# A two-layer encoder in fp32: the feed-forward moves to row order, its tokens are normalised in place from pair 3 on, and GpSimd's pair splits come in halves

## The chip, the cores and the metric

The kernel runs on one core of a Trainium2 chip (trn2). The metric is the device time of one execution in microseconds (us), the median of three runs. Engines are named as the profile names them: PE is TensorE's matmuls, PEld its weight loads, DVE VectorE, ACT ScalarE, POOL GpSimd, SP SyncE, which issues nearly all DMAs.

## What is computed

Two layers on 512 tokens (8 rows of 64 columns) of width 1024, each with three residual parts, and a last RMSNorm. Cut to what matters here:

```python
def conv_ffn(h, w_up, conv_w, conv_b, w_down):
    u = h @ w_up                                  # 1024 -> 2 x 2816
    up = jnp.pad(u, ((0, 0), (1, 1), (0, 0)))
    u = up[:, :-2] * conv_w[0] + up[:, 1:-1] * conv_w[1] + up[:, 2:] * conv_w[2] + conv_b
    gate, val = jnp.split(u, 2, axis=-1)
    return (jax.nn.silu(gate) * val) @ w_down

for l in range(DEPTH):                            # DEPTH = 2
    x = x + hybrid_mixer(rms_norm(x, norm_mix[l]), ...)      # neighbourhood and grouped-query attention
    x = x + memory_cross_attention(rms_norm(x, norm_mem_q[l]), rms_norm(mem, norm_mem_kv[l]), ...)
    x = x + conv_ffn(rms_norm(x, norm_ffn[l]), w_up[l], conv_w[l], conv_b[l], w_down[l])
return rms_norm(x, norm_final)
```

The convolution runs along the token index, which counts along a row of 64 columns first.

## The kernel before

Everything is held transposed: xT is eight chunks of 128 channels by 512 tokens. The tokens stand column by column (token = column x 8 + row), as the neighbourhood attention wants them, from the first load to the result, which the host puts back. In that order a token's neighbour in a row lies 8 elements away, and the first one of a row follows the last one of the row before across the whole tile. So each of the convolution's two outer taps is two instructions on VectorE (line 1826): one of 504 elements and one of 7.

Each fp32 matmul is made of three: both operands are split into a high part that TensorE takes as it is (ScalarE copies it, type fp32r) and a low part, the rest (VectorE or GpSimd subtracts), and high x high, high x low and low x high are added up in PSUM (`mm3`, `gemm_T`). The weights are split on the way in: `split_form` (line 746) does it for those of the forms described below, the low part on GpSimd or VectorE.

`Norm` keeps a residual's normalisation. When an output row m (128 channels) of the memory attention (`mem_rows`) or of the last part of the first layer's feed-forward (`down_closing`) is done in PSUM, `close` adds xT[m] in PSUM (line 974), copies the sum to xT[m] (975), makes the high part on ScalarE (983) and the low part on VectorE (985) of the sum times the gain, into the tiles `xg`, and squares it (ScalarE, added up by GpSimd). The reciprocal root of the mean square is not known then; it is multiplied in later.

The feed-forward of a layer goes over 22 pairs of column blocks (128 gate columns and 128 value columns each), in groups of 6, 6, 5 and 5; between the pairs of a group the rows of `down` for the group before are computed. Pairs 0 to 5 (`PLAIN` = 6) are plain products: `up_project` for both sides from `xg`, then `up_finish` multiplies both by the spread reciprocal root `ffn.rep` (line 1809), then `convolve`: ScalarE does the middle tap with the bias, VectorE the outer taps, ScalarE the SiLU, VectorE the product, and the result is split for `down`.

From pair 6 on `up_forms` computes a pair by seven products of half the tokens and half the channels instead of eight. It needs normalised tokens and sums of them, so in pairs 2 to 5 `token_forms` makes xn = xT x gain x reciprocal root (line 1846, eight chunks in four tiles) and then four sums and differences of quarters of it, t1, t3, t2 and t4, each split (lines 1856 to 1859); just before pair 6 `split_tokens` splits xn itself (lines 1870 and 1871) over the tiles `xg`, which the plain pairs no longer need. In `up_forms` the accumulator `first` is read by the addition on line 1903 and then written further by the last product ("val" with t4); that product waits for the addition.

The order of the instructions on ScalarE, VectorE, GpSimd and TensorE is not the order of this text. A planner (class `Order`, line 328) runs a model of the engines with costs by operation and size, and fixes each engine's order when the kernel is built. Its costs know nothing of the step between elements. SyncE's DMAs stay in the written order.

Of the kernel before, what the change touches and what calls it, by code (L numbers as in the profile page):

```python
# [20 lines left out]
S = 512  # L21
D = 1024
DEPTH = 2
GW = 64
# [13 lines left out]
PLAIN = 6  # L38
FIRST_ROWS = 2
# [614 lines left out]
def encoder_kernel(ctx: ExitStack, tc: tile.TileContext, t: dict, out: bass.AP):  # L654
# [91 lines left out]
    def split_form(src, n, act, eng):  # L746
        hi = wpool.tile([P, 2 * n, P], F32R, tag="hi", name=nm("hi"), padded_shape=[P, KC, P])
        lo = wpool.tile([P, 2 * n, P], F32R, tag="lo", name=nm("lo"), padded_shape=[P, KC, P])
        act.copy(hi, src)  # L749
        eng.tensor_sub(lo, src, f(hi))  # L750
        return hi, lo
# [207 lines left out]
    class Norm:  # L959


        def __init__(self, gcol=None, l=None, cols=slice(0, S)):
            self.gcol, self.l, self.acc, self.last, self.cols, self.n = gcol, l, None, [], cols, cols.stop - cols.start
            if gcol is not None:
                self.hi, self.lo = [xpool.tile([P, KC, S], F32R, tag="xg", name=nm("xg"), bufs=2) for _ in range(2)]
                self.ops = [(self.hi[:, c, :], self.lo[:, c, :]) for c in range(KC)]
# [4 lines left out]
        def close(self, c, pm):  # L971


            DVE.tensor_add(pm, pm, xT[c])
            DVE.tensor_copy(xT[c], pm)
            self.operand(c, src=pm)
            self.square(c)

        def operand(self, c, act=ACT, src=None, dve=DVE, hi_only=False, lo_only=False):
            src = xT[c] if src is None else src  # L980
            g = self.gain(c)
            hi, lo = self.ops[c]
            e = None if lo_only else act.activation(hi, src, AF.Copy, scale=g)
            if not hi_only:
                dve.scalar_tensor_tensor(lo, src, g, f(hi), op0=ALU.mult, op1=ALU.subtract)
            return e
# [162 lines left out]
    for l in range(DEPTH):  # L1149
# [615 lines left out]
        nn = Norm(G_FFN, l)  # L1765
# [35 lines left out]
        def up(j):  # L1801
            if j >= PLAIN:
                up_forms(j)
                return
            up_finish(j, [up_project(j, side) for side in range(2)])
# [6 lines left out]
        def convolve(j, us):  # L1812
            cs = []
            for side in range(2):
# [5 lines left out]
                for wi, dst, src in (  # L1820
                    (w[0], slice(8, S), slice(0, S - 8)),
                    (w[0], slice(1, 8), slice(S - 8, S - 1)),
                    (w[2], slice(0, S - 8), slice(8, S)),
                    (w[2], slice(S - 8, S - 1), slice(1, 8)),
                ):
# [15 lines left out]
        def token_forms():  # L1841
# [3 lines left out]
            for c in range(KC):  # L1845
                DVE.scalar_tensor_tensor(xn[c // 2][:, c % 2], xT[c], ffn.gain(c), ffn.psum, op0=ALU.mult, op1=ALU.mult)
                if c == 3:
                    yield
            yield
            made = {}  # L1850
            for name, a, b in (("t1", (0, 1), (0, 0)), ("t3", (1, 1), (0, 1)), ("t2", (1, 1), "t1"), ("t4", (1, 0), "t2")):
# [9 lines left out]

        def split_tokens():


            for name, k, n in (("b11", 0, 0), ("b21", 1, 0), ("b22", 1, 1)):
                xform[name] = [v[:, 4 * k : 4 * k + 4, halves[n]] for v in (ffn.hi, ffn.lo)]
            for c, n in ((0, HALF), (2, HALF), (4, S), (6, S)):
                hi, lo = (v[:, c : c + 2, :n] for v in (ffn.hi, ffn.lo))
                src = xn[c // 2][:, :, :n]
                ACT.copy(hi, src)  # L1870
                DVE.tensor_sub(lo, src, f(hi))  # L1871
# [108 lines left out]
        for what, n, rows in sequence():  # L1980
            if what == "down":
                down(n, rows)
            elif n == 0:
                up_first()
            elif n > 1:
                if n < PLAIN:
                    next(forms, None)
                elif n == PLAIN:
                    for _ in forms:
                        pass  # L1990
                    split_tokens()
                up(n)
        if l + 1 < DEPTH:
            nn = Norm(G_MIX, l + 1)
# [88 lines left out]
```

## Time and profile before

| | |
|---|---|
| median of 3 runs | 1325.12 us (1324.66 to 1325.38) |
| profiled execution, its own time | 1324.98 us |
| span of that execution, first to last instruction | 1323.2 us |
| TensorE busy | 1306.0 us, 99% |
| VectorE / ScalarE / GpSimd busy | 1004.2 / 783.4 / 724.9 us |
| granted TensorE clock, mean | 0.996 |
| HBM traffic | 97 GB/s over the span |

The page and the views of the trace give start and length of instructions in us from the span's start, the line in the kernel, the operation, output and inputs by the program's names, sizes as partitions x elements, and in brackets how long the engine was idle before and what ended that. In a view by groups the columns are count, busy us, mean ns of one, and idle us before them. A busy TensorE is one with matmuls in flight, not one at its peak rate.

### The profile page before, as it was taken

The page shows a single profiled execution, that of the slowest core. Times are in us where ns is not written, and L with a number is a line of the kernel's source. Part 1 is how long each engine was busy: PE and PEld are TensorE (multiplying, and loading weights), DVE is VectorE, ACT ScalarE, POOL GpSimd, SP SyncE. Part 2 cuts the span into 40 slices and gives each one's busy share as a digit, 9 for nine tenths or more (in the row PEclk, how much of TensorE's full clock was granted, in tenths as well). Part 3 has the DMA queues.
Part 4 walks back from the last instruction along what each step waited for, and adds up shares of the span by engine and source line. Part 5 has one row for each costly group of instructions (what it writes and reads, how often), then busy time and mean ns, then how long its engine had stood idle before and what let it go on. Part 6 is the DMA issues. An engine that isn't in the chain of part 4 may idle for free.

```text
span 1323.2 us, 21017 instructions
## 1 busy us (share of the span) xinstructions
PE 1306.0 (99%) x7632; PEld 1150.3 (87%) x7632; DVE 1004.2 (76%) x1862; ACT 783.4 (59%) x1450; POOL 724.9 (55%) x520
## 2 busy tenths in 40 slices
PE   9999999999999999999999999999999899999998
PEld 8888888888879999999888888888888899999987
DVE  7569877665998987788545698786758998877874
ACT  6768776565555555555536688765645455555544
POOL 3657965717464544454646579655454544444443
PEclk9999999999999999999999999999999999999999
DMA  8734222313213333333455533232232233333332
GB/s 245 188 120 133 97 79 65 99 44 112 88 50 97 106 112 103 99 101 93 137 156 165 150 90 96 56 89 80 64 90 74 69 108 104 101 97 93 116 98 76
DMA packets 205000, 136.98 MB, mean 104 GB/s; under 512 B 5600, under 2 KB 195040, under 8 KB 204896
## 3 DMA queue, kind: packets, MB, share of 16 engines
q1 hardware_dynamic: 204080, 134.98, 34.7%
q8 instruction: 60, 0.98, 0.3%
q10 hardware_dynamic: 816, 0.66, 0.2%
q14 instruction: 44, 0.36, 0.1%
HBM read 125.65 MB, written 2.10 MB: 97 GB/s over the span
## 4 chain that ended last, share of the span: by engine, by line
PE 91%; DVE 5%; ACT 2%; DMA 1%; issue 1%; POOL 0%; POOLq 0%; SPq 0%; ACTq 0%; DVEq 0%
PE mm L101 62%; PE sc L101 21%; PE tr L101 4%; PE tr L1533 2%; DVE xg L1871 1%; PE tr L1378 1%; DVE r L1856 1%; DMA r<-in_bias 1%; DVE r L1031 1%; PE tr L1720 1%; DMA raw<-in_w_in 0%; ACT t L1356 0%; DVE r L1248 0%; DVE sc L1350 0%; ACT r L1227 0%
## 5 line engine op out<-in xcount | busy, mean ns | idle before, releaser
L741 POOL TENSOR_TENSOR lo<-raw,hi 128x512 fp32r<-128x512 f32 (+3 forms) x230 | 371.3, 1629 | 291.2 <-ACT hi L740 243.5
L101 PE MATMUL mm<-r,hi 128*128 128x512 f32 (+1 forms) x1392 | 398.8, 367 | 0.0
L101 PEld LDWEIGHTS mm<-r,hi 128*128 128x128 f32 x1392 | 245.7, 190 | 34.9
L101 PE MATMUL mm<-xg,hi 128*128 128x512 f32 (+1 forms) x960 | 266.5, 363 | 0.5 <-ACT t L1897 0.3
L101 PE MATMUL mm<-r,lo 128*128 128x512 f32 (+1 forms) x728 | 257.9, 356 | 0.0
L740 ACT CAST hi<-raw 128x512 fp32r<-128x512 f32 (+3 forms) x234 | 167.9, 739 | 130.0 <-PE mm L101 52.3
L101 PEld LDWEIGHTS mm<-xg,hi 128*128 128x128 f32 x960 | 170.5, 189 | 27.3 <-issue 1.0
L101 PE MATMUL mm<-xg,lo 128*128 128x512 f32 (+1 forms) x480 | 173.5, 361 | 0.0
L101 PE MATMUL sc<-r,hi 128*128 128x256 f32 (+1 forms) x832 | 165.9, 294 | 5.7 <-DVE sc L1903 5.0
L750 POOL TENSOR_TENSOR lo<-sf,hi 128x1024 fp32r<-128x1024 f32 x32 | 79.1, 2473 | 140.2 <-ACT hi L749 117.0
L101 PEld LDWEIGHTS mm<-r,lo 128*128 128x128 f32 x728 | 137.9, 189 | 19.8
L101 PEld LDWEIGHTS sc<-r,hi 128*128 128x128 f32 x832 | 135.6, 193 | 12.2 <-issue 3.1
L101 PE MATMUL sc<-r,lo 128*128 128x256 f32 (+1 forms) x416 | 122.0, 293 | 0.0
L101 PE MATMUL mm<-hi,xg 128*128 128x512 f32 (+1 forms) x384 | 111.5, 360 | 2.6 <-DVE r L1231 1.3
L749 ACT CAST hi<-sf 128x1024 fp32r<-128x1024 f32 x64 | 67.1, 1050 | 78.8 <-DVE sf L762 46.3
L750 POOL TENSOR_TENSOR lo<-raw,hi 128x1024 fp32r<-128x1024 f32 x32 | 78.1, 2439 | 47.9 <-ACT hi L749 32.9
L101 PEld LDWEIGHTS mm<-xg,lo 128*128 128x128 f32 x480 | 90.6, 189 | 14.2 <-POOL lo L750 0.2
L1037 POOL TENSOR_SCALAR t<-t,s 128x512 f32<-128x512 f32 (+1 forms) x112 | 66.4, 607 | 52.6 <-DVE s L1517 27.7
L101 PEld LDWEIGHTS sc<-r,lo 128*128 128x128 f32 x416 | 80.4, 193 | 1.3
L101 PEld LDWEIGHTS mm<-hi,xg 128*128 128x128 f32 x384 | 68.1, 189 | 11.8 <-DVE r L1231 1.5
L101 PE MATMUL sc<-r,r 128*128 128x256 f32 (+1 forms) x352 | 74.6, 331 | 0.0
L101 PE MATMUL mm<-lo,xg 128*128 128x512 f32 (+1 forms) x192 | 68.5, 357 | 0.0
(200 smaller groups left out, 2615.5 us busy)
## 6 DMA issues: line engine op xcount, KB each, us to landing
raw<-in_w_up SPq DMA_DIRECT2D x88, 512.0 KB, 3.7
raw<-in_w_down SPq DMA_DIRECT2D x36, 384.0 KB, 3.3
raw<-in_w_in SPq DMA_DIRECT2D x25, 512.0 KB, 4.5
raw<-in_w_mem_kv SPq DMA_DIRECT2D x16, 512.0 KB, 4.2
raw<-in_w_down SPq DMA_DIRECT2D x24, 320.0 KB, 3.1
r<-in_bias SPq DMA_DIRECT2D x16, 384.0 KB, 4.8
r<-r SPq DMA_DIRECT2D x22, 256.0 KB, 3.5
raw<-in_w_in SPq DMA_DIRECT2D x18, 256.0 KB, 4.6
```

Of the source, the lines that this page charges most:

```text
L101: return self.engine.matmul(out, lhsT, rhs, **k)
L740: act.copy(hi[:, k], raw[:, k])
L741: (POOL if eng[0] == "P" else DVE).tensor_sub(lo[:, k], raw[:, k], f(hi)[:, k])
L749: act.copy(hi, src)
L750: eng.tensor_sub(lo, src, f(hi))
L1031: DVE.tensor_sub(lo, ps, f(hi))
L1037: eng.tensor_scalar(e, e, sums[:, col : col + 1], 1.0, op0=ALU.mult, op1=ALU.mult)
L1378: PE.transpose(tr[:, (2 * i + c) * P : (2 * i + c + 1) * P], es[j][:, i, c * P : (c + 1) * P], ident)
L1533: PE.transpose(tr[:, k * P : (k + 1) * P], es[j][:, k * P : (k + 1) * P], ident)
L1720: PE.transpose(tr[:, (2 * c + i) * P : (2 * c + i + 1) * P], e[:, i, c * P : (c + 1) * P], ident)
L1856: (POOL if name == "t3" else DVE).tensor_sub(made[name][:, k], quarter(*a)[i], other)
L1871: DVE.tensor_sub(lo, src, f(hi))
```

## The change

Three parts:

1. The feed-forward works on tokens in row order (row x 64 + column). `Norm` gets an argument `turn`; with it the copy to xT and both parts of the operand are written through a rearranged view (`turned`), so that the sum in PSUM, in column order, lands in row order ("rows", both layers, after the memory attention), and back ("columns", once, at the close of the first layer's feed-forward). An outer tap of the convolution becomes one instruction of 511 elements. The last layer's result leaves in row order, and the host only transposes it.
2. xn is made after pairs 0 and 1 (`scale_tokens`), and all of it is split over `xg` before pair 3 (`SCALED` = 3). Pairs 3, 4 and 5 multiply these tokens, without the multiplication by `ffn.rep`. The sums of tokens are made one each before pair 3 and after pairs 3, 4 and 5, in the order t1, t2, t3, t4.
3. In `split_form` GpSimd's subtraction comes in two halves (`CUTS` = 2).

```diff
--- before.py
+++ after.py
@@ -36,6 +36,8 @@
 PLAIN = 6
+SCALED = 3
+CUTS = 2
 FIRST_ROWS = 2
 HALF = S // 2
 EPS = 1e-6
@@ -747,7 +749,9 @@
         hi = wpool.tile([P, 2 * n, P], F32R, tag="hi", name=nm("hi"), padded_shape=[P, KC, P])
         lo = wpool.tile([P, 2 * n, P], F32R, tag="lo", name=nm("lo"), padded_shape=[P, KC, P])
         act.copy(hi, src)
-        eng.tensor_sub(lo, src, f(hi))
+        for i in range(CUTS if eng is POOL else 1):
+            c = slice(2 * n * i // CUTS, 2 * n * (i + 1) // CUTS) if eng is POOL else slice(0, 2 * n)
+            eng.tensor_sub(lo[:, c], src[:, c], f(hi)[:, c])
         return hi, lo
     def form_gate(raw, act):
@@ -959,7 +963,8 @@
     class Norm:
-        def __init__(self, gcol=None, l=None, cols=slice(0, S)):
+        def __init__(self, gcol=None, l=None, cols=slice(0, S), turn=None):
+            self.turn = turn
             self.gcol, self.l, self.acc, self.last, self.cols, self.n = gcol, l, None, [], cols, cols.stop - cols.start
             if gcol is not None:
                 self.hi, self.lo = [xpool.tile([P, KC, S], F32R, tag="xg", name=nm("xg"), bufs=2) for _ in range(2)]
@@ -972,14 +977,24 @@
             DVE.tensor_add(pm, pm, xT[c])
-            DVE.tensor_copy(xT[c], pm)
+            DVE.tensor_copy(*self.turned(xT[c], pm))
             self.operand(c, src=pm)
             self.square(c)
+
+        def turned(self, new, old):
+
+            if self.turn == "rows":
+                return new.rearrange("p (r c) -> p c r", r=ROWS), old.rearrange("p (c r) -> p c r", r=ROWS)
+            if self.turn == "columns":
+                return new.rearrange("p (c r) -> p r c", r=ROWS), old.rearrange("p (r c) -> p r c", r=ROWS)
+            return new, old
         def operand(self, c, act=ACT, src=None, dve=DVE, hi_only=False, lo_only=False):
             src = xT[c] if src is None else src
             g = self.gain(c)
             hi, lo = self.ops[c]
+            if self.turn:
+                (hi, src), (lo, _) = self.turned(hi, src), self.turned(lo, src)
             e = None if lo_only else act.activation(hi, src, AF.Copy, scale=g)
             if not hi_only:
                 dve.scalar_tensor_tensor(lo, src, g, f(hi), op0=ALU.mult, op1=ALU.subtract)
@@ -1762,7 +1777,7 @@
                 gemm_T(*rows[m][:2], mo, [3], 0, 3, rows[m][2])
                 nn.close(m, rows[m][0])
-        nn = Norm(G_FFN, l)
+        nn = Norm(G_FFN, l, turn="rows")
         fill = Filler(PE, late, mem_project(0, 1), mem_project(2), mem_project(3), mem_rows())
         fill.step(6)
         mq.stat(128.0)
@@ -1802,7 +1817,7 @@
             if j >= PLAIN:
                 up_forms(j)
                 return
-            up_finish(j, [up_project(j, side) for side in range(2)])
+            (up_finish if j < SCALED else convolve)(j, [up_project(j, side) for side in range(2)])
         def up_finish(j, us):
             for u in us:
@@ -1817,12 +1832,7 @@
                 w = [par[:, l, CW + i * 2 * NF + ch : CW + i * 2 * NF + ch + 1] for i in range(3)]
                 cc = tmp()
                 ACT.activation(cc, u, AF.Identity, bias=par[:, l, CB + ch : CB + ch + 1], scale=w[1])
-                for wi, dst, src in (
-                    (w[0], slice(8, S), slice(0, S - 8)),
-                    (w[0], slice(1, 8), slice(S - 8, S - 1)),
-                    (w[2], slice(0, S - 8), slice(8, S)),
-                    (w[2], slice(S - 8, S - 1), slice(1, 8)),
-                ):
+                for wi, dst, src in ((w[0], slice(1, S), slice(0, S - 1)), (w[2], slice(0, S - 1), slice(1, S))):
                     DVE.scalar_tensor_tensor(cc[:, dst], u[:, src], wi, cc[:, dst], op0=ALU.mult, op1=ALU.add)
                 cs.append(cc)
             ACT.activation(us[0], cs[0], AF.Silu)
@@ -1838,17 +1848,29 @@
         def quarter(k, n):
             return [xn[2 * k + i][:, :, halves[n]] for i in range(2)]
-        def token_forms():
+        def scale_tokens():
             xn.extend(rtile((2, S), F32) for _ in range(4))
             for c in range(KC):
                 DVE.scalar_tensor_tensor(xn[c // 2][:, c % 2], xT[c], ffn.gain(c), ffn.psum, op0=ALU.mult, op1=ALU.mult)
-                if c == 3:
-                    yield
-            yield
+
+        def split_tokens():
+
+
+            for c in range(KC):
+                hi, lo = ffn.ops[c]
+                src = xn[c // 2][:, c % 2]
+                ACT.copy(hi, src)
+                DVE.tensor_sub(lo, src, f(hi))
+            for name, k, n in (("b11", 0, 0), ("b21", 1, 0), ("b22", 1, 1)):
+                xform[name] = [v[:, 4 * k : 4 * k + 4, halves[n]] for v in (ffn.hi, ffn.lo)]
+
+        def token_forms():
+
+
             made = {}
-            for name, a, b in (("t1", (0, 1), (0, 0)), ("t3", (1, 1), (0, 1)), ("t2", (1, 1), "t1"), ("t4", (1, 0), "t2")):
+            for name, a, b in (("t1", (0, 1), (0, 0)), ("t2", (1, 1), "t1"), ("t3", (1, 1), (0, 1)), ("t4", (1, 0), "t2")):
                 src = made[name] = rtile((4, HALF), F32)
                 for i in range(2):
                     k = slice(2 * i, 2 * i + 2)
@@ -1858,17 +1880,6 @@
                 ACT.copy(hi, src)
                 (POOL if name in ("t2", "t3") else DVE).tensor_sub(lo, src, f(hi))
                 yield
-
-        def split_tokens():
-
-
-            for name, k, n in (("b11", 0, 0), ("b21", 1, 0), ("b22", 1, 1)):
-                xform[name] = [v[:, 4 * k : 4 * k + 4, halves[n]] for v in (ffn.hi, ffn.lo)]
-            for c, n in ((0, HALF), (2, HALF), (4, S), (6, S)):
-                hi, lo = (v[:, c : c + 2, :n] for v in (ffn.hi, ffn.lo))
-                src = xn[c // 2][:, :, :n]
-                ACT.copy(hi, src)
-                DVE.tensor_sub(lo, src, f(hi))
         def up_forms(j):
@@ -1982,16 +1993,19 @@
                 down(n, rows)
             elif n == 0:
                 up_first()
+                scale_tokens()
             elif n > 1:
-                if n < PLAIN:
-                    next(forms, None)
+                if n == SCALED:
+                    split_tokens()
+                    next(forms)
                 elif n == PLAIN:
                     for _ in forms:
                         pass
-                    split_tokens()
                 up(n)
+                if SCALED <= n < PLAIN:
+                    next(forms, None)
         if l + 1 < DEPTH:
-            nn = Norm(G_MIX, l + 1)
+            nn = Norm(G_MIX, l + 1, turn="columns")
             down_closing(len(GROUPS) - 1)
         else:
             down_last()
@@ -2079,4 +2093,4 @@
         encoder_kernel(tc, t, out)
     r = run_bass_kernel_spmd(nc, [arrays], core_ids=[0])
     y = r.results[0]["out_0"]
-    return np.ascontiguousarray(y.reshape(D, GW, ROWS).transpose(2, 1, 0)).reshape(1, S, D)
+    return np.ascontiguousarray(y.T).reshape(1, S, D)
```

## The prediction

> **What bounds the kernel now.** I read the page's busy shares first, then TensorE's waits, then the engines' timelines around the longest of them, then the groups of instructions.
>
> ```profile
> span 1323.2 us, 21017 instructions
> PE 1306.0 (99%) x7632; PEld 1150.3 (87%) x7632; DVE 1004.2 (76%) x1862; ACT 783.4 (59%) x1450; POOL 724.9 (55%) x520
> ```
>
> TensorE (PE) is idle for 1323.2 - 1306.0 = 17.2 us. The change leaves every matmul as it is, so VectorE (DVE) work that it saves is worth something only where TensorE waits for it. The waits by name:
>
> ```profile
> PE sc L101 <- DVE sc L1903: 5.0, 2, 2.7
> PE mm L101 <- DVE r L1231: 1.3, 1, 1.3
> PE mm L101 <- DVE r L1248: 1.3, 1, 1.3
> PE sc L101 <- POOL r L1859: 0.5, 1, 0.5
> PE mm L101 <- ACT t L1897: 0.3, 1, 0.3
> ```
>
> The first is the largest: once a layer, in the first pair of output columns that is computed by forms (pair 6), TensorE waits for the addition on line 1903. The timelines of VectorE, GpSimd (POOL) and TensorE in the first layer show why it is late:
>
> ```profile
> 382.08 7.37 DVE L1871 TENSOR_TENSOR xg<-r,xg 128x512 fp32r<-128x512 f32 x3
> 389.37 2.94 DVE L1856 TENSOR_TENSOR r<-r,r 128x512 f32<-128x512 f32 x2
> ...
> 393.43 0.42 DVE L1903 TENSOR_TENSOR sc<-sc,t 128x256 f32<-128x256 f32 x1
> 382.19 2.83 POOL L1859 TENSOR_TENSOR r<-r,r 128x1024 fp32r<-128x1024 f32 x1 [3.52 <-ACT r L1858]
> 384.98 3.38 POOL L750 TENSOR_TENSOR lo<-sf,hi 128x1024 fp32r<-128x1024 f32 x1
> 391.38 0.28 PE L101 MATMUL sc<-r,lo 128*128 128x256 f32 x1
> 393.99 0.35 PE L101 MATMUL sc<-r,hi 128*128 128x256 f32 x1 [2.33 <-DVE sc L1903]
> ```
>
> VectorE is inside the token split (line 1871) for 7.37 us, because each of these subtractions reads two SBUF operands while GpSimd runs one of its own. The clock that TensorE is granted falls right after both long waits, and not around the two of 1.3 us, which lie in the first two of these windows (columns: length, then busy time and count of PE, PEld, DVE, ACT and POOL, clock, DMA):
>
> ```profile
> 33.00:41.00 8.00, 6.74 (x56) 6.53 (x55) 5.99 (x10) 6.96 (x13) 2.03 (x3) 1.00 0.42 107
> 70.00:79.00 9.00, 7.71 (x42) 6.42 (x41) 5.62 (x14) 5.91 (x15) 5.93 (x7) 1.00 0.62 188
> 394.00:399.10 5.10, 5.07 (x22) 4.45 (x23) 4.48 (x8) 1.11 (x2) 2.81 (x1) 0.67 0.65 179
> 1047.00:1052.10 5.10, 5.06 (x22) 4.54 (x23) 3.89 (x8) 2.61 (x3) 0.00 (x0) 0.67 0.46 134
> ```
>
> A mean of 0.67 over 5.10 us loses 0.33 x 5.10 = 1.7 us of full-speed work, in each layer.
>
> **Gain: the jam ahead of the first forms pair.** Waits 5.0, clock 2 x 1.7 = 3.4, and the two short waits of the same stage 0.5 + 0.3: together 9.2 us. The split moves ahead of pair 3, and the sums t1, t2 and t3 to pairs 3 to 5. In the built program's order only t4 (two subtractions and a split) still stands before pair 6 on VectorE. Without the 7.37 us VectorE would come to the addition near 386, 5 us before TensorE's 391.38, so next in line are the products themselves. I take all 9.2; the bounds are 0, if other work refills the queue, and those 9.2.
>
> [...]
>
> **Cost: closing rows into turned tokens.** After the memory attention each of eight rows is closed by three VectorE instructions: add in PSUM (line 974), copy to xT (975), low part (985). The last two, and ScalarE's high part (983), now write SBUF with a step of 64 words from element to element. No row has such a write. The nearest rows:
>
> ```profile
> L975 DVE COPY xT<-mm 128x512 f32<-128x512 f32 x32 | 21.5, 685 | 0.3
> L985 DVE SCALAR_TENSOR_TENSOR xg<-mm,par,xg 128x512 fp32r<-128x512 f32 x32 | 23.6, 746 | 7.0 <-ACT xg L983 6.7
> L1628 DVE TENSOR_REDUCE t<-mm 128x256 f32<-128x512 f32 x8 | 5.5, 684 | 1.6 <-PE mm L101 1.6
> L761 DVE TENSOR_TENSOR sf<-raw 128x512 f32<-128x512 f32 x32 | 50.8, 1588 | 11.5 <-DMA raw<-in_w_up 11.4
> 293.00:311.00 18.00, 18.00 (x81) 14.90 (x80) 15.30 (x25) 13.23 (x20) 14.87 (x9) 1.00 0.30 88
> 306.25 1.40 DVE L985 SCALAR_TENSOR_TENSOR xg<-mm,par,xg 128x512 fp32r<-128x512 f32 x2
> 305.93 0.62 PE L101 MATMUL mm<-xg,hi 128*128 128x512 f32 x2
> ...
> 310.01 0.62 PE L101 MATMUL mm<-xg,hi 128*128 128x512 f32 x2
> ...
> 310.69 0.62 PE L101 MATMUL mm<-xg,hi 128*128 128x512 f32 x2
> ```
>
> Call the added time of such an instruction x. The reduction on line 1628 hops through PSUM at every element and takes 684 ns for 512, as much as the plain copy: x = 0. The slowest mean of a 512-wide VectorE instruction is 1588 ns: x = 1588 - 685 = 0.9 us. A gain is excluded, since neither instruction loses elements. I take x = 0.3, nearer to the first end, because 1588 ns holds waiting for GpSimd, which these writes don't have, and still above it, since a read of PSUM is not a write of SBUF.
>
> What x does: VectorE works through this stage almost without a pause. Chunk 6's low part ends at 306.25 + 1.40 = 307.65, and TensorE wants it with the second matmul of the row at 310.01, at 310.24: slack 2.6 us. Seven copies and seven low parts stand up to it on VectorE, all behind one another, so TensorE comes 14x - 2.6 late, and nothing under x = 0.19. The order of this stage is the same in both programs and both layers. At 0.3: 1.6 us a layer, 3.2 in all; at 0.9: 20 in all. The waits for a PSUM bank on the way (a row's bank comes free with its low part) are part of the same lateness. ScalarE has 18.00 - 13.23 = 4.8 us free there: eight high parts, each 0.3 longer, take 2.4 of it.
>
> [...]
>
> Once, between the layers, tokens are turned back (step 8 words):
>
> ```profile
> 660.43 0.70 DVE L974 TENSOR_TENSOR mm<-mm,xT 128x512 f32<-128x512 f32 x1 [1.54 <-PE mm L101]
> ...
> 663.13 0.75 DVE L985 SCALAR_TENSOR_TENSOR xg<-mm,par,xg 128x512 fp32r<-128x512 f32 x1 [0.76 <-ACT xg L983]
> 664.99 0.62 PE L101 MATMUL sc<-xg,hi 128*128 128x512 f32 x2
> ```
>
> Rows come slowly here, so only the tail counts: the last low part ends at 663.88 and is wanted at 665.22, slack 1.3. Three strided instructions stand on that tail, and the program's order puts the last addition of squares (0.6) ahead of the low part: 3x + 0.6 - 1.3 = 0.2 us at 0.3, 2.0 at 0.9.
>
> **Cost: split ahead of pair 3.** The new wait is VectorE's, for pair 2's last read of each chunk; behind it in the queue stand pair 2's convolution and the next chunks, and TensorE waits for all eight.
>
> ```profile
> 332.97 0.69 DVE L1809 TENSOR_TENSOR mm<-mm,rep 128x512 f32<-128x512 f32 x1
> 340.84 0.61 PE L101 MATMUL mm<-xg,hi 128*128 128x512 f32 x2
> 343.34 2.40 POOL L741 TENSOR_TENSOR lo<-raw,hi 128x1024 fp32r<-128x1024 f32 x1 [3.06 <-ACT hi L740]
> L1809 DVE TENSOR_TENSOR mm<-mm,rep 128x512 f32<-128x512 f32 x24 | 16.4, 693 | 15.8 <-ACT rep L956 15.3 <-PE mm L101 0.4
> L1826 DVE SCALAR_TENSOR_TENSOR t<-mm,par,t 128x7 f32<-128x7 f32 x48 | 10.0, 215 | 0.0
> L750 POOL TENSOR_TENSOR lo<-sf,hi 128x1024 fp32r<-128x1024 f32 x32 | 79.1, 2473 | 140.2 <-ACT hi L749 117.0 <-PE mm L101 14.2 <-PE sc L101 9.1
> L741 POOL TENSOR_TENSOR lo<-raw,hi 128x512 fp32r<-128x512 f32 x130 | 169.2, 1324 | 94.1 <-ACT hi L740 86.6 <-issue 4.4 <-PE sc L101 2.3
> ```
>
> Pair 3 starts at 340.84 (144 matmuls after 305.93). After the multiplication that starts at 332.97, eleven instructions stand on VectorE up to and with the first chunk's subtraction (four taps, two multiplications, three scalings, two splits); at about 0.64 us each from one start to the next they end at 333.6 + 11 x 0.64 = 340.6. Wanted at 340.84 + 0.23: slack 0.5. Later chunks come every 1.25 us (a scaling and a subtraction) and are used every 1.36 (six matmuls; three take 310.69 - 310.01 = 0.68), as the new TensorE order interleaves both sides. So alone it costs nothing. Under GpSimd's 2.40-us split at 343.34 a subtraction waits up to 2.4 us, 1.2 in the mean: I take 1.2 a layer, 2.4 in all, bounds 0 and 4.8.
>
> **Edits with no cost on the path.** 176 taps of 7 elements (line 1826, 48 of them in the row above, 215 ns) and 12 multiplications (line 1809, 693 ns) go: 176 x 0.21 = 37 and 8 us of VectorE, all beside TensorE, which after the jam is not kept waiting by it; if that cover were gone they would be gains. GpSimd's halves take 2 x 1324 instead of 2473 ns, 0.18 us more each time, with the first half 1.1 us earlier; GpSimd is 55% busy and TensorE's only wait for it is the 0.5 above. The DMA issues keep their order.
>
> **The sum.** -9.2 + 2 x (14x - 2.6) + (3x - 0.7) + 2.4 = 31x - 12.7; at x = 0.3 it is -3.4 us. From the profiled execution's 1324.98 us (span 1323.2 and 1.8 around it, 0.14 under the median of 1325.12): 1321.6.
>
> **Rivals.** First, dear strides: the same places with x over 0.41, where the sum turns positive, over 0.5 slower by 0.2%. At 0.6: +5.9, 1330.9; at 0.9: +15.2, 1340. For it: nothing on VectorE has slack in the closing stage (15.30 busy of 18.00). Against it: line 1628 hops free of charge. [...] Second, free strides (x under 0.19): -9.2 + 2.4 = -6.8, 1318.2. Third, the split ahead of pair 3 becomes the jam: the same subtractions took 7.37 us for three under two GpSimd instructions, and then TensorE waits 2.6 us and loses 1.7 of clock in each layer, 8.6 instead of 2.4: +2.8, 1327.8. For it speaks the slack of 0.5, against it that GpSimd has one split there and not two. Fourth, the change does not do what it says at pair 6: t4 and the column sums of the weights keep VectorE late, the 9.2 stay: +5.8, 1330.8; against it stand the 5 us of margin.
>
> **Numbers.** Forecast (x from 0.19 to 0.41) 0.37, dear strides 0.36, free strides 0.12, split jam 0.08, jam stays 0.07. Within 0.2%, 2.65 us, is about what a measurement can tell from no change. Faster: free strides and four fifths of the forecast, 0.42. Slower: dear strides above 0.5 (0.25), the two jams 0.15: 0.40. Same: 0.18. The range runs from all gained with no lock waits and a little more (1315) to x = 0.8 (+12.1, 1337). Cases of both signs hold most; the forecast's own range is 1318 to 1325.
>
> **What would show it.** Right: no wait on the addition after the "diffs" product, no clock at 0.5 near 394 and 1047; copies and low parts of the close at about 1.0 us; waits of 1 to 2 us in chunk 4 to 6 of the first up product. Wrong: copies over 1.1 us, with TensorE waiting for xg by more than 3 us a layer; a wait of over 2 us at pair 3.

## The result and the profile after

The changed kernel takes 1331.52 us, median of 6 runs (1330.99 to 1332.89), and the kernel before 1325.27 beside it: ratio 1.0046, 95% interval 1.0033 to 1.0059. It is slower by 6.2 us; the forecast was 3.5 us faster. The profiled execution, the slowest of the six, took 1332.89 us with a span of 1331.1.

The page's first lines:

```profile
span 1331.1 us, 20964 instructions
PE 1310.3 (98%) x7632; PEld 1149.8 (86%) x7632; DVE 977.5 (73%) x1682; ACT 796.0 (60%) x1458; POOL 750.9 (56%) x584
```

VectorE has 27 us less to do, as intended, and TensorE is idle for 20.8 us instead of 17.2. TensorE's waits by name, the largest four:

```profile
PE sc L103 <- ACT xg L998: 2.7, 1, 2.7
PE mm L103 <- DVE xg L1000: 2.2, 3, 0.9
PE mm L103 <- ACT mm L1838: 1.9, 2, 1.0
PE sc L103 <- DVE xg L1000: 1.8, 3, 0.7
```

The 5.0 us for the addition behind the "diffs" product in pair 6 are gone (a later pair waits 0.5 us for it once). All but the third line are waits for the operands `xg` of a close.

Both programs run the same 7632 matmuls, nearly in the same order. So the start of the i-th matmul in one trace can be taken from that in the other; how much the difference grows over a stretch is what the stretch lost or won. In us, against the profile of before (the single edits are told below; the last column is the difference at the last matmul):

| kernel | up to 284 | rows closed, 284-336 | pairs 3-5, 336-387 | first forms pair, 387-416 | between layers, 643-692 | up to 929 | rows, 929-980 | pairs 3-5, -1032 | forms pair, -1071 | rest | all |
|---|---|---|---|---|---|---|---|---|---|---|---|
| after | 1.0 | 2.4 | 0.5 | -4.5 | **10.5** | -0.6 | 2.2 | 1.2 | -5.8 | 1.1 | 8.2 |
| rows turned only | -0.4 | 2.4 | 0.6 | -4.5 | 0.1 | -0.6 | 2.1 | 1.2 | -5.8 | 0.0 | -4.9 |
| no turn | -0.7 | -0.3 | 0.5 | -4.5 | 5.8 | -0.6 | -0.3 | 1.2 | -5.8 | 0.8 | -3.8 |
| hops on the PSUM side | -0.8 | -0.3 | 0.6 | -4.5 | 0.0 | -0.6 | -0.3 | 1.2 | -5.8 | 0.0 | -10.5 |
| part 1 alone | -1.0 | 2.4 | 0.8 | -2.7 | 12.5 | 0.9 | 2.9 | 0.0 | -0.1 | -0.1 | 15.7 |
| part 2 alone | -0.7 | 0.0 | 0.5 | -4.5 | 0.0 | 1.0 | 0.0 | 1.4 | -5.8 | 0.3 | -7.9 |
| part 3 alone | 0.0 | 0.0 | -0.7 | -4.3 | 3.1 | -0.2 | 0.0 | 0.0 | -5.5 | 0.0 | -7.7 |
| after without part 3 | 0.8 | 2.4 | -0.4 | -3.9 | 11.1 | -0.1 | 2.4 | 0.3 | -5.3 | 0.5 | 7.9 |

(416 to 643 is left out: nothing changes there by 0.1 us.) The first row is the whole result: one stretch, between the layers, costs more than the two forms pairs bring. Of the 1.0 us up to 284, 0.85 stand already in the first 25 us of the execution; the other kernels lie there between -1.0 and 0.8, so one us of such a row can be scatter.

What one strided instruction costs stands in the groups of VectorE and ScalarE (count, busy us, mean ns):

```profile
L1000 DVE SCALAR_TENSOR_TENSOR xg<-mm,par,xg 128x512 fp32r<-128x512 f32 x32 | 32.2, 1018 | 9.9 <-ACT xg L998 9.8
L980 DVE COPY xT<-mm 128x512 f32<-128x512 f32 x32 | 29.6, 956 | 0.3
L998 ACT ACTIVATE xg<-mm,par 128x512 fp32r<-128x512 f32 x32 | 31.6, 1001 | 11.3 <-DVE xT L980 11.3
L980 DVE COPY xT<-sc 128x512 f32<-128x512 f32 x8 | 7.1, 886 | 0.0
```

These means mix strided and straight ones. 24 of the 40 copies are strided (8 of the 40 read a bank of the other kind and have a row of their own, the last one). The copies' excess over the straight duration, (956 - 685) x 32 + (886 - 682) x 8 = 10.3 us, over 24 is 0.43 us each; the low parts give 0.42 in the same way, ScalarE's high parts 0.51. By recorded lengths the x of the prediction is 0.43, not 0.3. Between the layers (step of 8 words) the three are 0.47, 0.49 and 0.55 on the mean of the eight rows, in the other turn (64 words) 0.41, 0.39 and 0.49.

Between the layers, VectorE's timeline (first block), ScalarE's (second) and TensorE's (third):

```profile
655.11 0.69 DVE L979 TENSOR_TENSOR mm<-mm,xT 128x512 f32<-128x512 f32 x1
655.84 1.15 DVE L980 COPY xT<-mm 128x512 f32<-128x512 f32 x1
658.82 1.25 DVE L1000 SCALAR_TENSOR_TENSOR xg<-mm,par,xg 128x512 fp32r<-128x512 f32 x1 [1.83 <-ACT xg L998]
659.96 0.70 DVE L979 TENSOR_TENSOR mm<-mm,xT 128x512 f32<-128x512 f32 x1
660.70 1.13 DVE L980 COPY xT<-mm 128x512 f32<-128x512 f32 x1
663.66 1.21 DVE L1000 SCALAR_TENSOR_TENSOR xg<-mm,par,xg 128x512 fp32r<-128x512 f32 x1 [1.83 <-ACT xg L998]
```

```profile
657.02 0.63 ACT L1006 ACTIVATE t<-xT 128x512 f32<-128x512 f32 x1 [1.67 <-DVE xT L980]
657.56 1.23 ACT L998 ACTIVATE xg<-mm,par 128x512 fp32r<-128x512 f32 x1
```

```profile
664.93 0.50 PE L103 MATMUL sc<-xg,hi 128*128 128x512 f32 x1 [0.75 <-DVE xg L1000]
668.38 0.49 PE L103 MATMUL sc<-xg,hi 128*128 128x512 f32 x1 [2.72 <-ACT xg L998]
669.58 0.79 PE L103 MATMUL sc<-xg,hi 128*128 128x512 f32 x1 [0.71 <-DVE xg L1000]
671.60 0.79 PE L103 MATMUL sc<-xg,hi 128*128 128x512 f32 x1 [0.37 <-DVE xg L1000]
```

One row is one round through two engines: sum (655.11), copy (655.84), ScalarE's square (657.02) and high part (657.56), low part (658.82), and only then, since it stands behind the low part in VectorE's queue, the next row's sum (659.96). VectorE waits 1.83 us in each round. From low part to low part the round takes 663.66 - 658.82 = 4.84 us. In the profile of before it was 3.36:

```profile
653.45 0.75 DVE L985 SCALAR_TENSOR_TENSOR xg<-mm,par,xg 128x512 fp32r<-128x512 f32 x1 [1.27 <-ACT xg L983]
656.81 0.75 DVE L985 SCALAR_TENSOR_TENSOR xg<-mm,par,xg 128x512 fp32r<-128x512 f32 x1 [1.28 <-ACT xg L983]
```

TensorE finishes a row each 3.4 us (15 matmuls at 0.227 us; three start within 0.68). Before, the round just fitted; now each row falls 1.45 us further behind TensorE than the one before. TensorE stands for 0.75 + 2.72 + 0.71 + 0.37 = 4.6 us, and the clock falls behind it (columns as in the windows of the prediction):

```profile
665.58:669.00 3.42, 0.58 (x2) 0.19 (x1) 3.31 (x4) 2.38 (x4) 2.45 (x3) 1.00 0.41 118
669.00:679.24 10.24, 9.29 (x25) 7.21 (x26) 4.78 (x8) 3.13 (x5) 6.48 (x5) 0.51 0.56 168
```

A mean of 0.51 over 10.24 us is 5.0 us of full-speed work lost. Wait and clock are 9.6 of the stretch's 10.5 us. The two drops of 3.41 us of before, near 394 and 1047, are gone.

### The profile page after: what moved, and what is told of

It reads as the page before. It is cut to its first block, busy times and chain, and to the rows that moved or that the text cites. A ratio compares the mean times of both kernels' runs of the same rounds, so it can differ in the third digit from the quotient of the medians.

```text
span 1331.1 us, 20964 instructions
## 1 busy us (share of the span) xinstructions
PE 1310.3 (98%) x7632; PEld 1149.8 (86%) x7632; DVE 977.5 (73%) x1682; ACT 796.0 (60%) x1458; POOL 750.9 (56%) x584
## 5 line engine op out<-in xcount | busy, mean ns | idle before, releaser
L754 POOL TENSOR_TENSOR lo<-sf,hi 128x512 fp32r<-128x512 f32 x64 | 86.4, 1372 | 105.8 <-ACT hi L751 90.5
L754 POOL TENSOR_TENSOR lo<-raw,hi 128x512 fp32r<-128x512 f32 x64 | 97.4, 1541 | 44.0 <-ACT hi L751 34.4
L103 PE MATMUL sc<-xg,hi 128*128 128x256 f32 (+1 forms) x320 | 71.4, 318 | 4.5 <-ACT xg L998 2.7
```

Source lines behind the costliest of these rows:

```text
L103: return self.engine.matmul(out, lhsT, rhs, **k)
L754: eng.tensor_sub(lo[:, c], src[:, c], f(hi)[:, c])
```

## The experiments

Times of one batch stand beside their own runs of the kernel before, whose medians were 1324.19, 1324.27 and 1323.86 us. A ratio weighs all times of both kernels, so it need not be that of the two medians.

| kernel | median, us (range) | ratio to before, 95% interval |
|---|---|---|
| rows turned only | 1320.11 (1318.70 to 1328.62) | 0.9985 (0.9970 to 1.0000) |
| hops on the PSUM side | 1319.09 (1314.48 to 1319.91) | 0.9953 (0.9938 to 0.9968) |
| no turn | 1316.75 (1314.06 to 1321.77) | 0.9951 (0.9937 to 0.9966) |
| part 2 alone | 1318.88 (1316.85 to 1319.76) | 0.9959 (0.9947 to 0.9971) |
| operands scattered | 1323.20 (1321.60 to 1324.34) | 0.9992 (0.9983 to 1.0001) |
| high part scattered | 1317.74 (1317.36 to 1318.15) | 0.9952 (0.9936 to 0.9967) |
| strides priced in the planner | 1330.30 (1330.10 to 1331.55) | 1.0049 (1.0035 to 1.0063) |
| last square added by TensorE | 1316.66 (1316.13 to 1318.38) | 0.9946 (0.9933 to 0.9958) |
| last square in PSUM | 1314.45 (1313.71 to 1316.31) | 0.9925 (0.9912 to 0.9938) |
| after without part 3 | 1333.05 (1331.91 to 1336.19) | 1.0070 (1.0050 to 1.0089) |
| part 3 alone | 1317.02 (1313.68 to 1317.29) | 0.9937 (0.9921 to 0.9953) |
| part 1 alone | 1340.90 (1340.35 to 1341.25) | 1.0123 (1.0109 to 1.0136) |

### The turn back left out, both turns left out

```diff
-            nn = Norm(G_MIX, l + 1, turn="columns")
+            nn = Norm(G_MIX, l + 1)
```

> The changed kernel with the turn back to columns left out between the layers (layer 1 then works on tokens that stay in rows, so this part of the computation is left out); the turn to rows stays. Theory: the 10.2 us that the changed kernel lost between the layers come from the strided copy, high part and low part there, which make one row's chain of VectorE and ScalarE 4.85 us long over a pitch of 3.4 us on TensorE, and from the clock that drops behind the stall. Then this kernel takes 1331.5 - 10.2 = about 1321 us (1320 to 1323), no gap over 0.3 us stands in the rows between the layers, and the granted clock stays whole. Rival: the stall between the layers comes from the order in which the tokens' instructions are queued, or from the clock alone; then the time stays within 3 us of 1331.5 and the stall is still there.

Measured 1320.11, and the stretch between the layers is back at 0.1. The turn back is the 10.5 us. (Five of the twelve times lie at 1323 to 1329; no trace shows one of them.) Without the other turn too:

> The changed kernel with both turns left out (the convolution then takes neighbours in the order of rows as if they were columns' neighbours, so the computation of the neighbours is changed); token sums over three pairs and GpSimd's differences in two stay, the convolution keeps its two long taps. Theory: all that strided instructions cost is gone, 10.2 us between the layers and 2.4 us in each layer's rows: 1331.5 - 15 = about 1316.5 us (1315 to 1318). Rival: if the rows' 2.4 us a layer are a matter of the order or of the bank of the first pairs and not of strides, 1321.

Measured 1316.75. The rows' 2.4 and 2.2 us became -0.3 and -0.3, so they are strides altogether. The profiled execution nevertheless lost 5.8 us between the layers, with no strided instruction there. VectorE's timeline, TensorE's wait and the windows show a loss of another kind:

```profile
656.86 0.74 DVE L1000 SCALAR_TENSOR_TENSOR xg<-mm,par,xg 128x512 fp32r<-128x512 f32 x1
657.71 4.41 DVE L1017 TENSOR_TENSOR t<-t,t 128x512 f32<-128x512 f32 x1
662.05 0.74 DVE L1000 SCALAR_TENSOR_TENSOR xg<-mm,par,xg 128x512 fp32r<-128x512 f32 x1
```

```profile
PE sc L103 <- DVE xg L1000: 2.4, 1, 2.4
```

```profile
662.83:669.66 6.83, 6.82 (x20) 5.76 (x21) 1.60 (x5) 1.14 (x2) 1.39 (x1) 0.51 0.52 151
```

The last addition of squares (line 1017, two operands in SBUF, 0.69 us where GpSimd runs nothing beside it) took 4.41 us. GpSimd ran four differences without a pause from 656.57 to 661.57. The last low part stands behind the addition, TensorE waits 2.4 us for it, and 6.83 us run at 0.51.

### The hops moved to the PSUM side

```diff
             if self.turn == "rows":
-                return new.rearrange("p (r c) -> p c r", r=ROWS), old.rearrange("p (c r) -> p c r", r=ROWS)
+                return new.rearrange("p (r c) -> p r c", r=ROWS), old.rearrange("p (c r) -> p r c", r=ROWS)
             if self.turn == "columns":
-                return new.rearrange("p (c r) -> p r c", r=ROWS), old.rearrange("p (r c) -> p r c", r=ROWS)
+                return new.rearrange("p (c r) -> p c r", r=ROWS), old.rearrange("p (r c) -> p c r", r=ROWS)
```

> The changed kernel with the same two turns, but the instructions walk in the order of what they write: the hops of 8 or 64 words lie on the read of the PSUM bank, and the writes to SBUF are straight. Nothing is left out. Theory: only the strided write to SBUF costs (the convolution of before reads PSUM... the halves with a hop in the trace of before took no longer), so the copy falls back to about 0.69 us, the low part to 0.75 and the high part to 0.69; the loop of a row to 3.4 us; the time to 1331.5 - 10.2 - 4.8 = about 1316.5 us (1315 to 1319). Rival: a hop costs on either side; then the copies stay near 1.1 us, the loop near 4.8 and the time near 1331.

Only the order in which the elements are walked differs from the changed kernel. The groups:

```profile
L1000 DVE SCALAR_TENSOR_TENSOR xg<-mm,par,xg 128x512 fp32r<-128x512 f32 x32 | 23.4, 742 | 6.8 <-ACT xg L998 6.8
L980 DVE COPY xT<-mm 128x512 f32<-128x512 f32 x32 | 21.2, 682 | 0.3
L998 ACT ACTIVATE xg<-mm,par 128x512 fp32r<-128x512 f32 x32 | 21.6, 681 | 5.6 <-DVE xT L980 5.3
```

The hop on the read of PSUM is free on both engines: 682, 742 and 681 ns, as straight as before. The stretches fall to -0.3, 0.0 and -0.3. The median is 1319.09, at the upper edge of the expected 1315 to 1319, because four of six times lie near 1319; the profiled execution took 1314.48, just below it. What parts them is tried under "The last addition of squares" below.

### One or two of the three strided writes, between the layers only

Here the hops stay on the PSUM side, and between the layers the named instructions write with hops again, as in the change (`scattered`); the diff is that of the high and low part.

```diff
-                (hi, src), (lo, _) = self.turned(hi, src), self.turned(lo, src)
+                (hi, src), (lo, _) = self.scattered(hi, src), self.scattered(lo, src)
```

> The kernel with the hops on the PSUM side, but between the layers the high and the low part are written with hops again (step of 8 words), while the copy stays straight. Nothing is left out. Theory (a serial chain through VectorE and ScalarE sets the pace of the last rows between the layers): each row's chain grows by 0.5 us of the high part and 0.43 us of the low part, from about 3.4 to 4.3 us, over the last four rows 3.7 us, of which some 1.5 us of slack are free; TensorE then stands for 2 to 2.5 us behind the last rows, and where that empties a stretch of 3.41 us of the clock's count, the clock is halved for one or two such stretches, another 1.7 to 3.4 us: 2 to 6 us above the kernel with all hops on the PSUM side. Rival, the prediction's: rows come slowly enough there, only the tail of the last row counts, 0.9 us or nothing.

> The kernel with the hops on the PSUM side, but between the layers the high part alone, on ScalarE, is written with hops of 8 words. Nothing is left out. Theory (serial chain): VectorE's low part waits for the high part, so 0.5 us a row lands on the chain though ScalarE is idle for more than that in each row; over the last four rows 2.0 us, less some 1.5 us of slack: TensorE stands for 0 to 1 us more, and every low part between the layers starts about 0.5 us later behind its sum than in the kernel with straight writes. Rival, the prediction's: ScalarE has 4.8 us free there and its longer write is covered: the low parts start where they did.

The low parts of both (VectorE's timeline; high part alone, then high and low part):

```profile
651.38 0.75 DVE L1003 SCALAR_TENSOR_TENSOR xg<-mm,par,xg 128x512 fp32r<-128x512 f32 x1 [1.84 <-ACT xg L1001]
655.30 0.75 DVE L1003 SCALAR_TENSOR_TENSOR xg<-mm,par,xg 128x512 fp32r<-128x512 f32 x1 [1.83 <-ACT xg L1001]
```

```profile
652.95 1.24 DVE L1006 SCALAR_TENSOR_TENSOR xg<-mm,par,xg 128x512 fp32r<-128x512 f32 x1 [1.84 <-ACT xg L1004]
657.34 1.27 DVE L1006 SCALAR_TENSOR_TENSOR xg<-mm,par,xg 128x512 fp32r<-128x512 f32 x1 [1.84 <-ACT xg L1004]
```

The round is 3.92 us with the high part strided, 4.39 with the low part too, 4.84 with the copy too, against 3.36 with none: steps of 0.56, 0.47 and 0.45, where the lengths grew by 0.55, 0.49 and 0.47. Each instruction puts its whole excess on the round, ScalarE's as well, although ScalarE is idle for more than that. Between the layers the profiles lost 3.1 and 7.3 us against before, where the same kernel without these writes lost 0.0; 7.3 is above the expected 2 to 6 (the medians lie 4.1 apart, within it), and the prediction's rule would have given 0.9 or nothing. Of the 3.1 us, TensorE's wait is 0.65; one drop of the clock as long as those of before (3.41 us at 0.50) would be another 1.7, an estimate. That wait is for the last low part (661.22), which stood behind an addition of squares of 1.39 us instead of 0.69, so the 3.1 us are not the strided high part's alone; the lengths of the rounds are free of that. In the medians the high part alone cannot be told from the kernel without it, whose times are spread by the addition above.

### The planner told the price

```diff
+        if self.engine in ("ACT", "DVE") and any(self.hops(v) for v in (*ins.ins, *ins.outs)):
+            extra = 500.0 if self.engine == "ACT" else 420.0
+            self.busy, self.takes = self.busy + extra, self.takes + extra
```

> The changed kernel, and the planner that orders the instructions is told that a copy, low part or high part with hops takes 0.42 us longer on VectorE and 0.50 us longer on ScalarE; so queues are reordered, nothing else. Nothing is left out. Theory (the chain within a row is serial, whatever the order): between the layers at least 6 of the 10.2 us stay lost, time 1325 to 1332. Rival: the loss came from an order made for straight writes (the square ahead of the high part, other work between); then most of the 10.2 us comes back, 1320 to 1323.

Here my theory fell. The median is 1330.30, as it said, but for another reason. Between the layers no gap of TensorE is over 0.45 us, the clock stays at 1.00 and the stretch costs 1.2 instead of 10.5 us, with the same long instructions. VectorE's timeline:

```profile
657.29 1.15 DVE L992 COPY xT<-mm 128x512 f32<-128x512 f32 x1
658.25 0.78 DVE L991 TENSOR_TENSOR mm<-mm,xT 128x512 f32<-128x512 f32 x1
659.06 1.15 DVE L992 COPY xT<-mm 128x512 f32<-128x512 f32 x1
660.29 1.29 DVE L1012 SCALAR_TENSOR_TENSOR xg<-mm,par,xg 128x512 fp32r<-128x512 f32 x1
661.43 0.73 DVE L991 TENSOR_TENSOR mm<-mm,xT 128x512 f32<-128x512 f32 x1
```

The next row's sum (658.25) and copy (659.06) now stand ahead of this row's low part (660.29), so ScalarE's part of the round lies beside VectorE's. VectorE's own 0.7 + 1.15 + 1.25 = 3.1 us a row fit the 3.4. The time went where the plan took VectorE to earlier sums in the other turn:

```profile
PE mm L103 <- DVE xg L1012: 7.2, 3, 4.2
```

There sums and copies of later rows stand ahead of the first low parts; TensorE waits 4.2 us in the first layer and 2.6 in the second, and behind the first of these waits, from 306.79 to 309.77, its matmuls start 0.43 us apart instead of 0.23. So the loss between the layers needs both: strided writes, and an order laid out for straight ones. The rival of this experiment was right on the stretch and wrong on the total.

### The last addition of squares

```diff
+            elif self.turn and c == KC - 1:
+                self.end = sq
...
-                self.rstd, self.var = rsqrt(sums(self.acc), nb, 1.0 / D, factor)
+                self.rstd, self.var = rsqrt(sums(*([self.acc, self.end] if self.turn else [self.acc])), nb, 1.0 / D, factor)
```

> The kernel with the hops on the PSUM side; behind a turn the last row's squares are no longer added on VectorE to the sum of the others (128x512, both operands in SBUF) but by TensorE, whose column sums take two operands: four more products of one column for each such norm. Nothing is left out. Theory: in the profile without turns this addition took 4.41 us instead of 0.69 beside four of GpSimd's differences in a row, TensorE stood 2.4 us for the low part queued behind it, and the clock was halved for 6.8 us; the kernel with the hops on the PSUM side has times at 1314.5 and at 1319.3 as the addition meets GpSimd or not. Then all times here lie at 1314 to 1315.5. Rival: the two times come from elsewhere, and this kernel shows both again.

Measured 1316.66, four of five times within 0.7 us: the spread is gone, as the theory said, but 1 to 2 us above the level that it gave. The extra products and an order of the whole program that came out differently may both bear on that; it stays open. Instead the addition was kept on VectorE with one operand in PSUM:

```diff
-            sq = tmp((self.n,)) if self.gcol is not None or c == 0 or c >= KC - 2 else ps_s()[:, : self.n]
+            wide = c < KC - 1 if self.turn else c == 0 or c >= KC - 2
+            sq = tmp((self.n,)) if wide or self.gcol is not None and not self.turn else ps_s()[:, : self.n]
```

> The kernel with the hops on the PSUM side; behind a turn ScalarE writes the last row's squares to a PSUM bank instead of SBUF, so that VectorE's addition of them reads one operand from PSUM. Nothing is left out. Theory: the addition of 4.41 us was VectorE standing for GpSimd because both read two SBUF operands; with one operand in PSUM it takes about 0.7 us always, without the four extra products of the previous attempt (1316.7): 1314 to 1316, times within 1.5 us of each other. Rival: GpSimd holds VectorE up whichever memory it reads; times at 1314.5 and 1319 again. Second rival: the bank is missed by TensorE at the start of the next stage, 1317 or more.

VectorE's timeline and GpSimd's of this kernel:

```profile
656.94 0.69 DVE L1018 TENSOR_TENSOR t<-t,sc 128x512 f32<-128x512 f32 x1 [0.74 <-ACT sc L1007]
```

```profile
656.01 5.07 POOL L743 TENSOR_TENSOR lo<-raw,hi 128x512 fp32r<-128x512 f32 x4
```

In the middle of four differences the addition takes 0.69 us, and GpSimd's four take 5.07 us, hardly more than the 5.00 beside the slow addition. The median is 1314.45, the fastest of all here and 9.4 us faster than the kernel before; the five times lie within 2.6 us, four of them within 0.9, where 1.5 was expected. Beside four of GpSimd's differences the addition thus took 4.41 us with two SBUF operands and 0.69 with one. But with two SBUF operands it need not stand: in the profile of the kernel with the hops on the PSUM side (1314.48 us) it came in ahead of the second of GpSimd's four differences, and those took 5.51 us instead of 5.00:

```profile
657.64 0.69 DVE L1017 TENSOR_TENSOR t<-t,t 128x512 f32<-128x512 f32 x1
656.46 5.51 POOL L743 TENSOR_TENSOR lo<-raw,hi 128x512 fp32r<-128x512 f32 x4
```

That this parts the times near 1314.5 from those near 1319 is what both remedies speak for; no trace of that kernel at 1319 shows it.

### The parts alone

Part 3 undone in the changed kernel (`CUTS = 1`):

> The changed kernel with GpSimd's pair differences whole again (the third part of the change undone). Nothing is left out. Theory: the split is worth nothing that can be measured here: 1331.5, within 2 us. Rival: halves let VectorE in between, so whole differences of 2.5 us and more hold up VectorE's sums and low parts: 1335 or more; second rival: each half's start costs, so whole is faster, 1328 or less.

1333.05, ratio 1.0070 against 1.0046 with the halves: the intervals overlap, so what the halves are worth beside part 2 is not told from nothing. Part 3 alone in the kernel before:

> The kernel before with the third part of the change alone: GpSimd's pair differences in two. Nothing is left out. Theory: no change, 1325 within 2 us. Rival: the halves let VectorE in at the first form pair, where before lost 4 to 5 us a layer: 1318 to 1321.

1317.02: the rival was right on the time, if a little high. The forms pairs win 4.3 and 5.5 us, about as much as part 2 brings, but not because VectorE is let in. VectorE (first block) is still held up: two token sums take 4.60 us, 1.28 undisturbed. The addition starts at 392.22, 1.2 us earlier than before (393.43), and TensorE (second block) now has rows of `down` to compute until the products into a bank `sc` go on at 393.23, without a wait:

```profile
383.20 4.60 DVE L1859 TENSOR_TENSOR r<-r,r 128x512 f32<-128x512 f32 x2
389.43 2.86 DVE L1862 TENSOR_TENSOR r<-r,r 128x1024 fp32r<-128x1024 f32 x1
392.22 0.42 DVE L1906 TENSOR_TENSOR sc<-sc,t 128x256 f32<-128x256 f32 x1
```

```profile
391.61 0.63 PE L102 MATMUL mm<-r,hi 128*128 128x512 f32 x2
393.23 0.40 PE L102 MATMUL sc<-r,hi 128*128 128x256 f32 x2
```

The 3.1 us between the layers are the addition of squares again, 3.71 us long in that profile. Part 2 alone:

> The kernel before with the second part of the change alone: tokens scaled in place and split ahead of the fourth pair, token sums over three pairs; no turns, the convolution in four pieces, GpSimd's differences whole. Nothing is left out. Theory: the jam ahead of the first form pair goes (-4.2 to -5.8 a layer by the comparison of the two traces) and about 1.2 us a layer is lost between the third and the fourth pair: 1325.3 - 11.0 + 2.3 = about 1316.5 us (1315 to 1319). Rival: the four pieces of the convolution keep VectorE so full (0.3 us more a chunk, 12 chunks in pairs 3 to 5) that the token sums come late again, and the time is 1320 to 1325.

In the profiled execution (1316.85) as expected, with a median of 1318.88 at the upper end; the forms pairs win 4.5 and 5.8. Part 1 alone:

> The kernel before with the first part of the change alone: both turns by strided writes, and the convolution with two long taps. Nothing is left out. Theory: the parts add: 10.2 us between the layers and 2.4 us in each layer's rows are lost, and the first form pair keeps most of its loss, less what the two long taps save VectorE: 1325.3 + 15.0 = about 1340 us, less at most 3 (1336 to 1341). Rival: the convolution's saving alone removes the loss ahead of the first form pair (4.2 and 5.8 us), 1330 to 1333.

1340.90, as the parts add up. By the profiles parts 1, 2 and 3 alone give 15.7, -7.9 and -7.7; together they would be 0.1 and are 8.2, since parts 2 and 3 remove the same wait of TensorE. (The medians are nearer to a sum: 17.0 - 5.3 - 6.8 = 4.9 against 6.2. That the gain is shared rests on the columns of the forms pairs, not on these totals.) Whether the halves could do it without the other order that the planner laid out for them stays open: order and halves were not tried apart.

## Why the prediction was wrong

**The step that failed** is the turn back: "Rows come slowly here, so only the tail counts", priced at 0.2 us and measured at 10.5. I took TensorE's pace for the rows' pace and charged the three strided instructions once. But VectorE's queue held each row's sum behind the last row's low part, and the low part behind ScalarE. That round took 3.36 us before against a pace of 3.4: no slack at all. The profile of before showed it, in the 1.27 and 1.28 us that VectorE waited for ScalarE ahead of two low parts in a row; I quoted only the last row, where VectorE waits for TensorE (1.54), and read slack from that one. Three excesses of 0.47, 0.55 and 0.49 us in each row made 4.84. Nor did I price the clock: a stall of 2.3 us had cost 1.7 us behind it in the lines I quoted, and here the emptier stretch cost 5.0. With x = 0.43 my own formula for the tail gives 0.6 us, so the size of x was not the fault.

**x** was 0.43 on VectorE and 0.51 on ScalarE instead of 0.3, by recorded lengths. My 0.3 was a choice between the free hop on the read and 0.9, and no row showed it; on VectorE the copies say 0.43 and the low parts 0.42. My bound of 0 from the reduction on line 1628 was a true measurement of another thing: a hop on the read, which stays free in the kernel with hops on the PSUM side (682, 742 and 681 ns).

**Closing rows** was forecast at 1.6 us a layer and measured at 2.4 and 2.2. The mechanism, lateness that adds up on a full VectorE, was right, and so was the slack. With x = 0.43 the formula gives 14 x 0.43 - 2.6 = 3.4, but in a queue without pauses a strided instruction adds less than its recorded length. VectorE's first three copies (before, then after) and the end of chunk 6's low part (after; before it was at 307.65):

```profile
296.38 1.88 DVE L975 COPY xT<-mm 128x512 f32<-128x512 f32 x3
```

```profile
297.41 2.98 DVE L980 COPY xT<-mm 128x512 f32<-128x512 f32 x3
311.56 2.20 DVE L1000 SCALAR_TENSOR_TENSOR xg<-mm,par,xg 128x512 fp32r<-128x512 f32 x2
```

The three copies take 1.10 us more, 0.37 each. From the first of them to chunk 6's low part VectorE needs 16.35 us instead of 11.27; these 5.1 us more, less the slack of 2.6, are 2.5. For this queue x was 0.36, between my 0.3 and 0.43.

**The jam** was forecast at -9.2 us in all and gave -4.5 and -5.8: right, clock included. But the halves, which I put among the edits with no cost or gain, take TensorE's wait away by themselves, with the order that comes with them.

**The split ahead of pair 3** was forecast at 1.2 us a layer; the stretch cost 0.5 and 1.2. The wait shown there is not the one I named: TensorE waits 0.95 us for ScalarE's line 1838, the SiLU that is written to a PSUM bank, and not for a subtraction under GpSimd. The kernel with the last square in PSUM, which has another order, has no such wait (its stretches are -0.7 and 0.0).

**The rivals.** "Dear strides" began at x = 0.41, and x was 0.43; its total of 1330.9 lies near the result by luck: it was worked out for x = 0.6 by the same formula, without the round and the clock, and at 0.43 it gives +0.6 us in all. Without the turn back the sum of the measured terms is 8.2 - 10.5 = -2.3 us, where the forecast without that term was -3.6.

## What to carry to other kernels

Where two engines hand a tile back and forth, follow one round through both queues, in their order, and compare its length with the pace of what feeds it: if the round is as long as the pace (here 3.36 against 3.4 us), each instruction in it counts for every tile, also on an engine that is mostly idle (here 0.55 us more on ScalarE made the round 0.56 longer). When data must be reordered on the way from PSUM to SBUF, walk in the order of the write and let the read hop (here 682, 742 and 681 ns, against 1.05 to 1.31 us with the hops on the write in the changed kernel). An order laid out by a planner is only good for the durations it was given: after an edit that changes a duration, give it the new one, and look at every place that it then reorders.

## What the runs showed of the hardware

A hop on the write to SBUF lengthened a 128x512 fp32 copy or low part on VectorE by 0.47 to 0.49 us with a step of 8 words and by 0.39 to 0.41 with 64, and a high part on ScalarE by 0.55 and 0.49; the same hops on the read of PSUM cost nothing on either (682, 742 and 681 ns). Where VectorE's queue ran without a pause, such an instruction (step 64) held up those behind it by 0.36 us only; where another engine waited for it, its whole excess counted (rounds longer by 0.56, 0.47 and 0.45 us).

In one run an addition with two SBUF operands did not get between GpSimd's instructions and took 4.41 us, until all that were left of the four were done; in another, started at nearly the same place among them (1.2 us behind the start of the first, instead of 1.1), it took 0.69. With one operand in PSUM it took 0.69 in the middle of them. The profile of before shows the same parting. The addition on line 761, 128x512 with two SBUF operands, took 0.68 to 0.69 us in the seven of its 32 times that had no GpSimd instruction beside them, and up to 2.88 (from 1259.63, beside a GpSimd subtraction from 1259.56) in the others; of the 7.37 us of token split on line 1871 two subtractions of 128x1024 took 3.42 each, where one in the second layer, begun just ahead of GpSimd's (1032.41 against 1032.45), took 1.21. With one operand in PSUM the 40 additions of line 974 took 0.69 to 0.70 us and the 40 low parts of line 985 0.74 to 0.75, though GpSimd was at work for more than half of 32 and of all 40 of them.

The granted clock fell behind stretches of 3.41 us in which TensorE was busy for a part only: for 1.62 and for 0.72 us ahead of the two drops of before (3.41 us each at 0.50, from 395.65 and from 1047.60), for 0.58 of 3.42 us ahead of the changed kernel's 10.24 us. In the kernel without turns, with this stretch ahead of it, the clock was down for 6.83:

```profile
659.40:662.81 3.41, 1.06 (x5) 0.56 (x3) 3.38 (x2) 0.00 (x0) 2.17 (x2) 1.00 0.51 159
```

10.24 and 6.83 are three and two times 3.41 us. No drop followed the stretches from 71.38 and 33.84 in the profile of before, in which TensorE was busy for 2.12 and 2.15 us of 3.41.
